# VectorE on constant addresses, one relu per 16 rows: a change beside a full DMA queue

## The chip, the cores and the metric

One core of one Trainium2 chip. The metric is device time in microseconds (us). A profiled run also has a span, from the first to the last instruction of the core that the profile shows; the time is longer than the span, by 1.30 to 1.73 us in the means below, and the difference of the two matters in this case. Every run quoted here was in the fast state, at a granted clock of 1.0.

## The reference

RMSNorm with relu, 16 x 1024 rows of 512 fp32 elements:

```
rms = sqrt(mean(x ** 2, axis=-1) + eps)
out = maximum(x / rms * gamma, 0)
```

33.5 MB are read and 33.5 MB written; per element there is a handful of operations.

## The kernel before

Rows are cut into eight chunks of 16 rows for each of the 128 partitions (4.19 MB), which share six slots in SBUF. SP issues all loads and stores in one queue, in this order: chunks 0 to 5 in, 0 and 1 out, 6 and 7 in, 2 to 7 out. ScalarE squares and sums each row, and takes a root for each eight rows. VectorE makes the factor, multiplies row by row, and clamps. ScalarE and VectorE run loops with addresses in registers. (`take` waits for a semaphore and counts it down in one instruction of its own, in the trace one `EVENT_SEMAPHORE` of 21 ns on VectorE.)

```
    with nc.vector.Fori(0, ngroups) as gi:            # 16 groups of 8 rows
        take(nc.vector, sq, 1)
        base = nc.vector.snap((gi % (nslots * per)) * (G * d))
        col = nc.vector.snap(gi * G)
        ...
        nc.vector.reciprocal(out=rstd[...], in_=rms[...]).then_inc(sv, 1)
        take(nc.vector, sv, 1)
        for j in range(G):
            row = slots[:, bass.ds(base + j * d, d)]
            r = nc.vector.scalar_tensor_tensor(out=row, in0=row, scalar=rstd[...], in1=gamma_sb, ...)
            if j == 0: r.then_inc(tick1, 1)
            if j == 2: r.then_inc(tick3, 1)
            ...
        take(nc.vector, sv, 1)
        nc.vector.tensor_scalar_max(out=blk, in0=blk, scalar1=0.0).then_inc(done, 1)
```

SP does not release a store as soon as its chunk is done, but at two moments that VectorE's rows mark, the ticks:

```
    nc.sync.wait_ge(tick3, 6)          # third row of the sixth group
    store(0)
    store(1)
    for s in range(2):
        nc.sync.wait_ge(sem_slot[s], 32)
        load(7 + s)                    # chunks 6 and 7
    nc.sync.wait_ge(tick1, 11)         # first row of the eleventh group
    for i in range(2, nchunks):
        store(i)
```

## Time and profile before

| | before |
|---|---|
| time, median of 4 runs of the comparison | 160.62 us |
| span of the profiled run | 159.3 us |
| DMA: share of 16 engines, mean rate | 98.2%, 421 GB/s |
| VectorE, ScalarE busy | 126.0 us, 86.3 us |
| last clamp ends, last store issued | 146.44, 146.47 us |

### The profile page before, as it was taken

The numbers are of one execution on the slowest core, as the hardware profiler recorded it, in microseconds if no ns is written. First come the engines' busy times: TensorE is split into PE (matmuls) and PEld (weight loads), VectorE is DVE, ScalarE is ACT, GpSimd is POOL, SyncE is SP. The second block draws the span as 40 slices with busy tenths as digits, with TensorE's granted clock in tenths as the row PEclk, the third lists the DMA queues.
The fourth block names the chain that finished last, engine by engine and source line by source line (L and its number), as shares of the span: only waits on it lengthen the run. The fifth ranks groups of instructions, "written<-read, shape, count | busy, mean of one in ns | idle before, by whom it ended". The sixth has DMA issues, their size and how long they took to land. (4 is left out here: it accounts for less than half of the span.)

```text
span 159.3 us, 999 instructions
## 1 busy us (share of the span) xinstructions
DVE 126.0 (79%) x164; ACT 86.3 (54%) x273; POOL 0.2 (0%) x4
## 2 busy tenths in 40 slices
DVE  1012989898999999999999999999999989897000
ACT  0388929889989988988920098898500000000000
POOL 0000000000000000000000000000000000000000
DMA  6999999999999999999999999999999999999995
GB/s 193 405 453 424 502 395 395 502 420 395 453 469 395 395 502 420 395 428 494 395 395 444 461 411 395 486 436 395 453 453 403 411 494 411 403 461 453 395 420 247
DMA packets 2456, 67.12 MB, mean 421 GB/s; under 512 B 276, under 2 KB 276, under 8 KB 280
## 3 DMA queue, kind: packets, MB, share of 16 engines
q1 hardware_dynamic: 2448, 67.11, 98.2%
q10 hardware_dynamic: 8, 0.01, 0.0%
HBM read 33.56 MB, written 33.55 MB: 421 GB/s over the span
## 5 line engine op out<-in xcount | busy, mean ns | idle before, releaser
L157 DVE SCALAR_TENSOR_TENSOR slots<-slots,rstd,gamma_sb 128x512 f32 x128 | 86.2, 747 | 4.8 <-DVEq L83 4.8
L136 ACT ACTIVATE junk<-slots 128x512 f32 x128 | 74.4, 581 | 20.6 <-ACTq L83 20.3
L167 DVE TENSOR_SCALAR slots<-slots x16 | 36.7, 2294 | 2.4 <-DVEq L83 0.2
L136 ACT ACTIVATION_READ_ACCUMULATOR junk<-slots x128 | 23.9, 187 | 0.0
L152 DVE RECIPROCAL rstd<-rms x16 | 3.1, 197 | 5.3 <-DVEq L83 5.3
L142 ACT ACTIVATE rms<-ss,eps_sb x16 | 4.8, 301 | 3.0 <-ACTq L83 3.0
L146 DVE LOAD_MASK_SELECT gamma_sb<-gseed x1 | 0.0, 14 | 5.4 <-DVEq L83 5.4
L129 ACT ACT_TABLE_LOAD x1 | 1.3, 1283 | 4.2 <-issue 4.2
L122 DVE MEMSET gseed<- 128x512 f32 x1 | 0.5, 485 | 2.6 <-PEq L98 2.6
L146 DVE STREAM_SHUFFLE gamma_sb<-gseed 128x512 f32<-128x512 f32 x1 | 0.7, 723 | 0.0
L190 POOL MEMSET const-bfloat16-1.0<- 128x1 bf16 x1 | 0.1, 102 | 0.0
L190 POOL MEMSET const-uint8-127<- 128x1 uint8 x1 | 0.1, 102 | 0.0
L190 POOL MEMSET const-float32-0.0<- 128x1 f32 x1 | 0.1, 99 | 0.2 <-issue 0.2
L190 POOL MEMSET const-float32-1.0<- 128x1 f32 x1 | 0.1, 99 | 0.0
L123 DVE MEMSET eps_sb<- 128x1 f32 x1 | 0.1, 59 | 0.0
## 6 DMA issues: line engine op xcount, KB each, us to landing
out_dram<-slots SPq DMA_DIRECT2D x8, 4096.0 KB, 20.6
slots<-in_x_dram SPq DMA_DIRECT2D x7, 4096.0 KB, 29.7
slots<-in_x_dram SPq DMA_DIRECT2D x2, 2048.0 KB, 9.7
gseed<-in_gamma_dram ACTq DMA_DIRECT2D x1, 8.0 KB
```

Source lines behind the costliest of these rows:

```text
L122: nc.vector.memset(gseed, 0.0).then_inc(sem_z, 1)
L123: nc.vector.memset(eps_sb, eps).then_inc(sem_z, 1)
L129: nc.scalar.preload_act_table(ACTF.Sqrt)
L136: a = nc.scalar.activation(out=junk[:, j, :], in_=slots[:, bass.ds(base + j * d, d)], func=ACTF.Square, accum_out=ss[:, bass.ds(col + j, 1)])
L142: nc.scalar.activation(out=rms[:, bass.ds(col, G)], in_=ss[:, bass.ds(col, G)], func=ACTF.Sqrt, bias=eps_sb, scale=inv_d).then_inc(sq, 1)
L146: nc.vector.stream_shuffle(gamma_sb, gseed, [0] * 32)
L152: nc.vector.reciprocal(out=rstd[:, bass.ds(col, G)], in_=rms[:, bass.ds(col, G)]).then_inc(sv, 1)
L157: r = nc.vector.scalar_tensor_tensor(out=row, in0=row, scalar=rstd[:, bass.ds(col + j, 1)], in1=gamma_sb, op0=ALU.mult, op1=ALU.mult)
L167: nc.vector.tensor_scalar_max(out=blk, in0=blk, scalar1=0.0).then_inc(done, 1)
L190: nc = _bacc.Bacc("TRN2", target_bir_lowering=False, num_devices=1)
```

## The change

VectorE's rows go to constant addresses: all six slots are written out, and a loop of two turns runs them (in the second turn only slots 0 and 1). Factors are made by 16 rows except in these two slots, and the clamp covers 16 rows (chunk 2 keeps two of eight). The ticks become single marks on chosen rows. The seed memset goes to GpSimd. ScalarE's loop leaves chunks 5 and 7 to constant code. Both programs are now long (VectorE's from 45 to 142 instructions, ScalarE's from 50 to 135), and an alignment (`addr_align`) stands before each.

```
+    for engine in (nc.scalar, nc.vector):
+        engine.addr_align(256, offset=128, max_nops=0)
...
-    nc.sync.wait_ge(tick3, 6)
+    nc.sync.wait_ge(tick, 1)
...
-    nc.sync.wait_ge(tick1, 11)
+    nc.sync.wait_ge(tick, 2)
...
-    nc.vector.memset(gseed, 0.0).then_inc(sem_z, 1)
+    nc.gpsimd.memset(gseed, 0.0).then_inc(sem_z, 1)
...
-    with nc.vector.Fori(0, ngroups) as gi:
-        ... (the loop above)
+    with nc.vector.Fori(0, 2) as o:
+        chunk_rows(0, by_group=True)
+        chunk_rows(1, by_group=True)
+        one = steps
+        with nc.vector.If_lt(nc.vector.to_reg(o), 1):
+            chunk_rows(2, clamps=(G, K), ticked=13)
+            chunk_rows(3)
+            chunk_rows(4)
+            chunk_rows(5, ticked=6)
+            ...
```

(`chunk_rows(s)` writes out the reciprocal, 16 row operations and the clamp of slot s; `ticked` is the row that marks the tick; waits now stand on the operation itself.)

More of the change, by code (lines that the diff above doesn't have):

```diff
@@ L37 @@
     nslots = 6
-    ngroups = rows // G
     per = K // G
@@ L64 @@
     sq = nc.alloc_semaphore("sq")
-    tick1 = nc.alloc_semaphore("tick1")
-    tick3 = nc.alloc_semaphore("tick3")
+    tick = nc.alloc_semaphore("tick")
     done = nc.alloc_semaphore("done")
@@ L85, in store @@
     def store(i):
-        nc.sync.wait_ge(done, per * (i + 1))
+        nc.sync.wait_ge(done, i + 1)
         nc.sync.dma_start(out=ov[i], in_=slot_ap(i)).then_inc(sem_slot[i % nslots], 16)
-    ctx.enter_context(tc.manual_schedule(engines={mybir.EngineType.SP}))
+    ctx.enter_context(tc.manual_schedule(engines={
+        mybir.EngineType.SP, mybir.EngineType.Activation, mybir.EngineType.DVE}))
+    for engine in (nc.scalar, nc.vector):
+        engine.addr_align(256, offset=128, max_nops=0)
     early = 2
@@ L110 @@
         load(7 + s)
-    nc.sync.wait_ge(tick1, 11)
+    nc.sync.wait_ge(tick, 2)
     for i in range(2, nchunks):
         store(i)
+    nc.gpsimd.memset(gseed, 0.0).then_inc(sem_z, 1)
+    nc.gpsimd.memset(eps_sb, eps).then_inc(sem_z, 1)
     for m, (i, a, r) in enumerate(loads):
@@ L120 @@
         nc.gpsimd.sem_inc(ready, r // G)
-    nc.vector.memset(gseed, 0.0).then_inc(sem_z, 1)
-    nc.vector.memset(eps_sb, eps).then_inc(sem_z, 1)
     nc.scalar.wait_ge(sem_z, 1)
@@ L130 @@
     take(nc.scalar, sem_z, 2)
-    with nc.scalar.Fori(0, ngroups) as gi:
-        take(nc.scalar, ready, 1)
-        base = nc.scalar.snap((gi % (nslots * per)) * (G * d))
-        col = nc.scalar.snap(gi * G)
-        for j in range(G):
-            a = nc.scalar.activation(
-                out=junk[:, j, :], in_=slots[:, bass.ds(base + j * d, d)],
-                func=ACTF.Square, accum_out=ss[:, bass.ds(col + j, 1)])
-            if j == G - 1:
-                a.then_inc(sa, 1)
-        take(nc.scalar, sa, 1)
-        nc.scalar.activation(out=rms[:, bass.ds(col, G)], in_=ss[:, bass.ds(col, G)],
-                             func=ACTF.Sqrt, bias=eps_sb, scale=inv_d).then_inc(sq, 1)
@@ L145, with square @@
-    take(nc.vector, sem_g, 16)
-    nc.vector.stream_shuffle(gamma_sb, gseed, [0] * 32)
-    with nc.vector.Fori(0, ngroups) as gi:
-        take(nc.vector, sq, 1)
-        base = nc.vector.snap((gi % (nslots * per)) * (G * d))
-        col = nc.vector.snap(gi * G)
-        blk = slots[:, bass.ds(base, G * d)]
-        nc.vector.reciprocal(out=rstd[:, bass.ds(col, G)],
-                             in_=rms[:, bass.ds(col, G)]).then_inc(sv, 1)
-        take(nc.vector, sv, 1)
-        for j in range(G):
-            row = slots[:, bass.ds(base + j * d, d)]
+    def square(row, col, j):
+        return nc.scalar.activation(out=junk[:, j, :], in_=slots[:, bass.ds(row, d)],
+                                    func=ACTF.Square, accum_out=ss[:, bass.ds(col, 1)])
@@ new lines, in root, with chunk_sums @@
+    def root(col, r):
+        return nc.scalar.activation(out=rms[:, bass.ds(col, r)], in_=ss[:, bass.ds(col, r)],
+                                    func=ACTF.Sqrt, bias=eps_sb, scale=inv_d)
+    def chunk_sums(i):
+        c = (i % nslots) * K
+        take(nc.scalar, ready, per)
+        for j in range(K):
+            a = square((c + j) * d, c + j, j % G)
+            if j % G == G - 1:
+                a.then_inc(sa, 1)
+                nc.scalar.wait_ge(sa, (j + 1) // G)
+        root(c, K).then_inc(sq, per)
+        nc.scalar.sem_inc(sa, -per)
@@ new lines @@
+    with nc.scalar.Fori(0, 2) as o:
+        with nc.scalar.Fori(o * 12, o * 4 + 10) as gi:
+            take(nc.scalar, ready, 1)
+            col = nc.scalar.snap((gi % (nslots * per)) * G)
+            base = nc.scalar.snap(col * d)
+            for j in range(G):
+                a = square(base + j * d, col + j, j)
+            a.then_inc(sa, 1)
+            take(nc.scalar, sa, 1)
+            root(col, G).then_inc(sq, 1)
+        with nc.scalar.If_lt(nc.scalar.to_reg(o), 1):
+            chunk_sums(5)
+        with nc.scalar.Else():
+            chunk_sums(7)
@@ new lines, with factors, clamp, chunk_rows @@
+    nc.vector.wait_ge(sem_g, 16)
+    nc.vector.stream_shuffle(gamma_sb, gseed, [0] * 32)
+    steps = 0
+    def factors(c, r, n):
+        nc.vector.wait_ge(sq, n)
+        nc.vector.reciprocal(out=rstd[:, c:c + r], in_=rms[:, c:c + r]).then_inc(sv, 1)
+        nonlocal steps
+        steps += 1
+        nc.vector.wait_ge(sv, steps)
+    def clamp(c, r):
+        blk = slots[:, c * d:(c + r) * d]
+        return nc.vector.tensor_scalar_max(out=blk, in0=blk, scalar1=0.0)
+    def chunk_rows(s, by_group=False, clamps=(K,), ticked=None):
+        nonlocal steps
+        c = s * K
+        for j in range(K):
+            if by_group and j % G == 0:
+                factors(c + j, G, (c + j) // G + 1)
+            elif j == 0:
+                factors(c, K, per * (s + 1))
+            row = slots[:, (c + j) * d:(c + j + 1) * d]
@@ L157 @@
             r = nc.vector.scalar_tensor_tensor(
-                out=row, in0=row, scalar=rstd[:, bass.ds(col + j, 1)], in1=gamma_sb,
+                out=row, in0=row, scalar=rstd[:, c + j:c + j + 1], in1=gamma_sb,
                 op0=ALU.mult, op1=ALU.mult)
-            if j == 0:
-                r.then_inc(tick1, 1)
-            if j == 2:
-                r.then_inc(tick3, 1)
-            if j == G - 1:
-                r.then_inc(sv, 1)
-        take(nc.vector, sv, 1)
-        nc.vector.tensor_scalar_max(out=blk, in0=blk, scalar1=0.0).then_inc(done, 1)
@@ L169 @@
-    take(nc.sync, done, ngroups)
-    take(nc.sync, tick1, ngroups)
-    take(nc.sync, tick3, ngroups)
+            if j == ticked:
+                r.then_inc(tick, 1)
+            if j + 1 in clamps:
+                r.then_inc(sv, 1)
+                steps += 1
+                nc.vector.wait_ge(sv, steps)
+                k = clamps.index(j + 1)
+                n = j + 1 - (clamps[k - 1] if k else 0)
+                b = clamp(c + j + 1 - n, n)
+        b.then_inc(done, 1)
+    with nc.vector.Fori(0, 2) as o:
[7 more added lines that the diff above has]
+            chunk_rows(5, ticked=6)
+            nc.vector.sem_inc(sq, -nslots * per)
+            nc.vector.sem_inc(sv, -steps)
@@ L172 @@
+    take(nc.sync, done, nchunks)
+    take(nc.sync, tick, 2)
+    take(nc.sync, sem_g, 16)
+    take(nc.sync, sq, 2 * per)
+    take(nc.sync, sv, one)
     for i in range(nchunks - nslots, nchunks):
```

## The prediction

> **What bounds the kernel now.** I read the page's slices and queue table first, since they say which resource never rests, then the groups of instructions, then the waits of the DMA queue's engine (SP), and last the timeline of the tail.
>
> ```profile
> span 159.3 us, 999 instructions
> DVE 126.0 (79%) x164; ACT 86.3 (54%) x273; POOL 0.2 (0%) x4
> DMA  6999999999999999999999999999999999999995
> GB/s 193 405 453 424 502 395 395 502 420 395 453 469 395 395 502 420 395 428 494 395 395 444 461 411 395 486 436 395 453 453 403 411 494 411 403 461 453 395 420 247
> q1 hardware_dynamic: 2448, 67.11, 98.2%
> L157 DVE SCALAR_TENSOR_TENSOR slots<-slots,rstd,gamma_sb 128x512 f32 x128 | 86.2, 747 | 4.8 <-DVEq L83 4.8
> L167 DVE TENSOR_SCALAR slots<-slots x16 | 36.7, 2294 | 2.4 <-DVEq L83 0.2
> L152 DVE RECIPROCAL rstd<-rms x16 | 3.1, 197 | 5.3 <-DVEq L83 5.3
> ```
>
> The DMA row is 9 in all 40 slices but the first and the last, and the load/store queue has 98.2% of sixteen engines' time. The sawtooth of GB/s between 395 and 502 is packets being booked to the slice in which they start; over a long stretch it evens out, as the windows view shows:
>
> ```profile
> 0.00:8.00 8.00, 0.49 (x2) 1.28 (x1) 0.20 (x4) 1.00 0.78 300
> 8.00:58.00 50.00, 41.72 (x56) 42.70 (x137) 0.00 (x0) 1.00 1.01 435
> 102.00:146.00 44.00, 41.62 (x53) 10.93 (x35) 0.00 (x0) 1.00 1.01 438
> ```
>
> (Columns: stretch, length, busy us of VectorE, ScalarE and GpSimd with counts, clock, DMA share, GB/s.) The DMA share is full in the middle. Every byte is needed: 33.56 MB in, 33.55 MB out. So the DMA engines set the time, if they are never left without work. VectorE is at 79%, but a busy share does not show whether the last store waited for it. For that, the tail and SP's waits:
>
> ```profile
> 144.15 2.29 DVE L167 TENSOR_SCALAR slots<-slots  x1
> 146.47 0.33 SPq L87 DMA_DIRECT2D out_dram<-slots  x1
> ```
> ```profile
> SPq L83 <- SPq L83: 12.0, 2, 9.7
> ```
>
> VectorE's last clamp ends at 146.44 and store 7 is issued at 146.47, so that store did wait for VectorE. But was the queue empty? SP's last two waits (12.0 us together, the longest 9.7) are for stores 6 and 7. The span ends with the second, so store 6 landed at about 159.3 - 9.7 = 149.6. Store 7 was queued 3.1 us before store 6 had landed and took 9.7 us behind it: 4.19 MB in 9.7 us is 432 GB/s, the full rate again. The last store stood in the queue, not VectorE on the path. (The chain view names the last clamp for 1.4% of the span only; it is blind to a full queue.)
>
> [...] the clamp does 4096 elements in 2.29 us, the two-tensor row operation 512 in 0.75. [...] in the trace of before, no instruction packet lies after the span's start, so its loops cause none.
>
> **The change part by part.** One step of eight rows on VectorE, from the timeline of before:
>
> ```profile
> 22.74 0.20 DVE L152 RECIPROCAL rstd<-rms  x1
> 23.23 5.39 DVE L157 SCALAR_TENSOR_TENSOR slots<-slots,rstd,gamma_sb 128x512 f32 x8 [0.30 <-DVEq L83]
> 28.77 2.29 DVE L167 TENSOR_SCALAR slots<-slots  x1
> 30.98 0.20 DVE L152 RECIPROCAL rstd<-rms  x1
> ```
>
> Start to start: reciprocal to first row 0.49; a row (5.39 - 0.747)/7 = 0.663; last row to clamp 28.77 - 23.23 - 7 x 0.663 = 0.90; clamp to next reciprocal 2.21. A step is 8.24, sixteen are 131.9, and 14.48 (first reciprocal) + 131.9 = 146.4: the timeline's end, so VectorE is self-paced all the way.
>
> - Constant addresses remove eight register instructions a step. The trace has seven of them running ahead behind the first rows, hidden; only the one between wait and first row (115 ns) is exposed. So the row pitch stays 0.663, and reciprocal to first row falls to about 0.38. I choose 0.85 for last row to clamp, as the wait joins the clamp itself.
> - Factors: twelve reciprocals in place of sixteen (two in each of chunks 0, 1, 6 and 7, whose slots are the first two; one in chunks 2 to 5).
> - Clamps: nine in place of sixteen. A 16-row one should take 2.21 + 4096 x 0.52 ns = 4.34: the elements stay, only a wait and a start go.
> - Chunks 0, 1, 6, 7: 2 x 0.38 + 15 x 0.663 + 0.85 + 4.34 = 15.9 each, 63.6 in all. Chunk 2: 0.38 + 14 x 0.663 + 2 x 0.85 + 2 x 2.21 = 15.8. Chunks 3 to 5: 0.38 + 15 x 0.663 + 0.85 + 4.34 = 15.5 each, 46.5 in all. Sum 125.9: VectorE saves 6.0 us and ends at about 140.4.
> - ScalarE's two constant chunks save little, and ScalarE is not short: 0.61 us a row, 16 rows in about 11.5 us, under the 15.5 of VectorE. Chunk 2 now wants both of its roots at once. By ScalarE's pace of before the second ends at 45.9; VectorE arrives at about 46.3. No wait, narrowly. The second factor of chunk 0 is wanted at 20.2 and its root ends at 20.0: at most 0.1 us.
> - The seed memset goes to GpSimd. Gamma is shuffled at 8.4 and first needed at 15.0; a few us later would still be hidden.
>
> What reaches the end? Store 7 is issued 6 us earlier, into a queue that was already full. Saving: nothing. What could reach it is the moment of the first stores, which SP delays until the ticks:
>
> ```profile
> 58.30 0.82 SPq L87 DMA_DIRECT2D out_dram<-slots  x2
> 71.23 10.35 SPq L77 DMA_DIRECT2D slots<-in_x_dram  x2
> 98.19 48.62 SPq L87 DMA_DIRECT2D out_dram<-slots  x6
> ```
>
> The queue then runs dry near 61 and 100. The ticks move to row 14 of chunk 2 and row 7 of chunk 5. By my sums the first fires at 14.5 + 31.8 + (0.38 + 7 x 0.663 + 0.85 + 2.21) + 5 x 0.663 + 0.75 = 58.4, the second at 14.5 + 31.8 + 15.8 + 31.0 + 0.38 + 6 x 0.663 + 0.75 = 98.2. They are aimed at the old moments: more rows on a faster VectorE give the same time. So the order and moment of the first stores are as before, and the estimate is zero change: 160.5.
>
> **The rivals.** (1) *VectorE sets the end*, and its 6.0 us become 3 or more: about 155. For it, store 7 goes out straight after the last clamp; against it, 3.1 us of queue and 9.7 us at full rate, and the bytes alone: 67.11 MB at 435 GB/s are 154.3 us, to which a first packet near 1.7 and the half-empty end have to be added. (2) *A tick comes too late*, by a slower VectorE or a wait for a 16-row root, and the queue runs dry: each us of lateness costs up to a us. If my row pitch were off by 1%, the second tick would move by 0.6 us; SP needed 1.0 us from first issue (0.73) to first packet (1.75), so there is little in reserve. That gives 161 or so. (3) *Fetching instructions*: the longer program, or the jump over the alignment padding, adds packets to one DMA engine or stalls VectorE. [...] a fetch at the start is hidden behind the loads. At worst some tenths. (4) *Slow packets at the start become fewer*: the first slice has only 193 GB/s, about a us lost; but the change leaves the first two loads and their barrier alone.
>
> **Range and chances.** The floor leaves no way to 157.3 (2% faster), and the dry-queue rival would need 3.2 us of gap for 2% slower. Runs of before span 160.47 to 160.72. I take 160.1 to 161.0: 0.4 down for a tidier queue end, 0.5 up for a late tick or a fetch.
>
> **What would show it.** Right: VectorE busy 122 to 124 us in fewer instructions, rows still at 0.66 us pitch, its end near 140, SP's stores at about 58.4 and 98.2, store 7 issued near 140, SP's last wait still 9.7 us, DMA share 98%, and the span within 0.4 us of 159.3. Wrong: a DMA slice below 9 in the middle (ticks), a wait of VectorE for a root at chunk 2, or a last wait of SP different from 9.7 us. A span under 158.5 would mean that the queue had hidden gaps that I took for full use.

(Cut marks stand where a passage said of the hardware what no trace or run of this case shows. No term of the sum is cut: it came to 125.9 us from VectorE's first reciprocal to its end, 6.0 us saved there, and zero change of the time, 160.5 us. Its rate for the longer clamp, 0.52 ns an element, is not in the trace of before, where every clamp has 4096 elements; the trace after shows it: 4426 ns for 8192 elements against 2294 for 4096, so 2132 ns for 4096 more. That the queue runs dry near 61 and 100 us fits the loads of chunks 5 and 7, done at 61.56 and 100.54 us in the kernel before. That a late tick costs up to its lateness, and that a fetch at the start is hidden, were estimates: in e13 a first tick 0.73 us later made the span 1.0 us longer, and what fetches cost is measured below.)

## The result, and the profile after

The changed kernel takes **161.42 us** (median of 4 runs, 161.22 to 161.52) against **160.62 us** before (160.47 to 160.97). The ratio is 1.0045, 95% interval 1.0025 to 1.0065: slower clear of noise, and outside the predicted range. A ratio is the mean time of one kernel's fast runs over that of the other's of the same rounds, so not quite the ratio of the medians.

The page of the changed kernel:

```profile
span 159.7 us, 714 instructions
DVE 124.0 (78%) x151; ACT 85.7 (54%) x271; POOL 0.8 (0%) x6
DMA  6999999999999999999999999999999999999993
q1 hardware_dynamic: 2448, 67.11, 98.0%
q14 instruction: 2, 0.02, 0.0%
DVE 55%; issue 3%; ACT 0%; DVEq 0%; ACTq 0%
L182 DVE TENSOR_SCALAR slots<-slots 128x8192 f32<-128x8192 f32 (+1 forms) x9 | 35.6, 3952 | 0.3
L175 DVE RECIPROCAL rstd<-rms 128x8 f32<-128x8 f32 (+1 forms) x12 | 2.6, 214 | 5.9 <-ACT rms L140 5.9
```

Two of these lines mislead and one tells. The chain of work now claims 55% for VectorE, though its last work ends 20 us before the span does. The DMA row looks as it did. The new line is `q14 instruction`: two packets of 8192 bytes, which the kernel before did not have in its span. It has 0.0% of the engines' time.

VectorE did what it was meant to do. Its timeline, one chunk:

```profile
15.01 0.20 DVE L175 RECIPROCAL rstd<-rms 128x8 f32<-128x8 f32 x1 [5.45 <-ACT rms L140]
15.24 5.39 DVE L193 SCALAR_TENSOR_TENSOR slots<-slots,rstd,gamma_sb 128x512 f32<-128x512 f32 x8
20.83 0.20 DVE L175 RECIPROCAL rstd<-rms 128x8 f32<-128x8 f32 x1 [0.19 <-ACT rms L140]
21.07 5.39 DVE L193 SCALAR_TENSOR_TENSOR slots<-slots,rstd,gamma_sb 128x512 f32<-128x512 f32 x8
26.50 4.43 DVE L182 TENSOR_SCALAR slots<-slots 128x8192 f32<-128x8192 f32 x1
```

Eight rows still take 5.39 us; reciprocal to first row is 0.23 in place of 0.49. And the tail, with SP's wait for its last two stores:

```profile
135.06 4.43 DVE L182 TENSOR_SCALAR slots<-slots 128x8192 f32<-128x8192 f32 x1
139.51 0.33 SPq L88 DMA_DIRECT2D out_dram<-slots  x1
```
```profile
SPq L84 <- SPq L84: 19.2, 2, 9.7
```

Store 7 is issued 7 us earlier, and again lands 9.7 us behind store 6. The gain stood in the queue, as foreseen. So where do 0.8 us come from? At the start, ScalarE's first square, which waits for the first half of chunk 0, comes 0.75 us later (first line before, second line after):

```profile
8.73 0.60 ACT L136 ACTIVATE junk<-slots 128x512 f32 x1 [3.27 <-ACTq L83]
```
```profile
9.48 0.60 ACT L136 ACTIVATE junk<-slots 128x512 f32 x1 [3.96 <-ACTq L84]
```

The trace's semaphore records say why. Each transfer's semaphore is raised sixteen times, which I read as once by each DMA engine. The median, the last but one and the last of the sixteen, in us:

```
transfer                 before                    after
chunk 0, first half      7.84   8.11   8.26        7.88   8.16   9.01
chunk 0, second half    12.69  12.96  13.00       12.74  12.98  13.71
load of chunk 5         61.27  61.52  61.56       61.32  61.55  62.29
load of chunk 7        100.22 100.45 100.54      100.18 100.42 101.54
store 2                109.89 110.17 110.46      109.91 110.15 111.25
store 7                158.18 158.53 159.23      158.19 158.75 159.63
```

The typical engine is where it was, to 0.05 us, from the first transfer to the last. **One** engine (the same one, as I read it; these records name none) is about 0.75 us later than the last one of before from the first half of chunk 0 on, and 1.0 us later at the load of chunk 7; the work that waits for a transfer starts behind its last engine: the first square 0.47 us after the sixteenth raise in both kernels (8.73 for 8.26, 9.48 for 9.01). By store 7 the difference has shrunk to 0.40 us, which is that of the two profiled spans: in the kernel before, too, one engine falls behind while the stores run, to 1.05 us behind the median. The two instruction packets start at 1.8 us (578 ns) and 3.8 us (328 ns), and a load packet that starts at 4.1 us takes 1125 ns instead of 611.

A second part is outside the span. Time minus span is 1.59 us in the changed kernel's four runs (1.52 to 1.67), and 1.33 in the kernel before (mean of 11 runs). One more 8192-byte instruction packet stands at 161.1 us, after the span's end. The 0.8 us are so about 0.5 in the span (159.8 against 159.3, medians of the runs) and 0.26 after it.

### The profile page after: what moved, and what is told of

Same layout as the page of the kernel before. It is cut to its first block, busy times and chain, and to the rows that moved or that the text cites. A ratio compares the mean times of both kernels' runs of the same rounds, so it can differ in the third digit from the quotient of the medians.

```text
span 159.7 us, 714 instructions
## 1 busy us (share of the span) xinstructions
DVE 124.0 (78%) x151; ACT 85.7 (54%) x271; POOL 0.8 (0%) x6
## 4 chain that ended last, share of the span: by engine, by line
DVE 55%; issue 3%; ACT 0%; DVEq 0%; ACTq 0%
DVE slots L193 40%; DVE slots L182 14%; DVE rstd L175 1%; ACT rms L140 0%; DVEq L207 0%; ACTq L140 0%; DVEq L217 0%
## 5 line engine op out<-in xcount | busy, mean ns | idle before, releaser
L193 DVE SCALAR_TENSOR_TENSOR slots<-slots,rstd,gamma_sb 128x512 f32<-128x512 f32 x128 | 86.0, 748 | 0.4
L136 ACT ACTIVATE junk<-slots 128x512 f32 (+1 forms) x128 | 74.5, 582 | 21.3 <-ACTq L84 20.8
L182 DVE TENSOR_SCALAR slots<-slots 128x8192 f32<-128x8192 f32 (+1 forms) x9 | 35.6, 3952 | 0.3
L136 ACT ACTIVATION_READ_ACCUMULATOR junk<-slots (+1 forms) x128 | 23.9, 187 | 0.0
L175 DVE RECIPROCAL rstd<-rms 128x8 f32<-128x8 f32 (+1 forms) x12 | 2.6, 214 | 5.9 <-ACT rms L140 5.9
L140 ACT ACTIVATE rms<-ss,eps_sb (+1 forms) x14 | 4.2, 302 | 2.4 <-ACTq L84 2.2
L119 POOL MEMSET gseed<- 128x512 f32 x1 | 0.5, 524 | 1.9 <-POOLq L102 1.9
```

Source lines behind the costliest of these rows:

```text
L119: nc.gpsimd.memset(gseed, 0.0).then_inc(sem_z, 1)
L136: return nc.scalar.activation(out=junk[:, j, :], in_=slots[:, bass.ds(row, d)], func=ACTF.Square, accum_out=ss[:, bass.ds(col, 1)])
L140: return nc.scalar.activation(out=rms[:, bass.ds(col, r)], in_=ss[:, bass.ds(col, r)], func=ACTF.Sqrt, bias=eps_sb, scale=inv_d)
L175: nc.vector.reciprocal(out=rstd[:, c:c + r], in_=rms[:, c:c + r]).then_inc(sv, 1)
L182: return nc.vector.tensor_scalar_max(out=blk, in0=blk, scalar1=0.0)
```

## The experiments

Theory F: instruction fetches, at the start by one DMA engine, and at the end after the span. Rivals: P, VectorE's new pace or the new program as such; C or T, the moments of the ticks. Sixteen kernels, five rounds each, each beside runs of the kernel before on the same chip. All gave correct results.

| run | time | before | ratio (95%) | span | time - span |
|---|---|---|---|---|---|
| changed kernel | 161.42 | 160.62 | 1.0045 (1.0025-1.0065) | 159.8 | 1.59 |
| e1 changed, no alignment | 161.88 | 160.66 | 1.0065 (1.0052-1.0078) | 160.6 | 1.30 |
| e2 before + alignments | 160.67 | 160.66 | 1.0003 (0.9990-1.0015) | 159.4 | 1.32 |
| e3 changed, VectorE aligned only | 161.43 | 160.66 | 1.0044 (1.0031-1.0057) | 159.9 | 1.57 |
| e4 changed, ScalarE aligned only | 161.82 | 160.66 | 1.0064 (1.0051-1.0077) | 160.5 | 1.30 |
| e5 before, ticks early | 161.14 | 160.72 | 1.0024 (1.0011-1.0038) | 159.8 | 1.34 |
| e6 changed, both ticks late | 162.36 | 160.72 | 1.0092 (1.0078-1.0105) | 160.6 | 1.67 |
| e7 changed, both ticks early | 162.99 | 160.72 | 1.0142 (1.0126-1.0157) | 161.5 | 1.62 |
| e8 short program | 161.16 | 160.72 | 1.0031 (1.0017-1.0045) | 159.4 | 1.71 |
| e9 short program, aligned | 161.10 | 160.73 | 1.0017 (1.0004-1.0030) | 159.8 | 1.31 |
| e10 short program, inner loop | 166.50 | 160.73 | 1.0364 (1.0351-1.0377) | 165.2 | 1.31 |
| e11 before + tail on VectorE | 161.15 | 160.73 | 1.0021 (1.0008-1.0034) | 159.4 | 1.73 |
| e12 before + fetch in the stream | 161.24 | 160.73 | 1.0031 (1.0018-1.0044) | 159.9 | 1.33 |
| e13 changed, first tick late | 162.48 | 160.57 | 1.0114 (1.0099-1.0129) | 160.8 | 1.68 |
| e14 changed, second tick late | 160.96 | 160.57 | 1.0023 (1.0009-1.0037) | 159.3 | 1.65 |
| e15 e2, first tick earlier | 160.81 | 160.57 | 1.0018 (1.0005-1.0032) | 159.5 | 1.33 |
| e16 e9, second tick later | 160.96 | 160.57 | 1.0030 (1.0016-1.0045) | 159.6 | 1.32 |

(Spans are medians of the runs of that kernel, recorded to 0.1 us, and the last column has means; the kernel before has 159.3, 159.4, 159.4 and 159.2 in the four groups, and 1.31 to 1.33 after the span.)

### e1, e3, e4: the alignments taken away

```
e1  -    for engine in (nc.scalar, nc.vector):
    -        engine.addr_align(256, offset=128, max_nops=0)
e3  -    for engine in (nc.scalar, nc.vector):
    +    for engine in (nc.vector,):
e4  -    for engine in (nc.scalar, nc.vector):
    +    for engine in (nc.scalar,):
```

> The changed kernel without the two address alignments (ScalarE and VectorE); nothing else differs. Theory F (instruction fetch): the jumps over the padding cause the two 8 KB instruction packets at 1.8 and 3.8 us, both on one DMA engine, which then runs 0.6 to 0.7 us behind the other fifteen, and a third packet after the end. Expected: no instruction packet at the start, chunk 0's second half complete at 13.0 instead of 13.7, span 159.3, time 160.6. Theory T (the ticks leave the queue dry): time stays at 161.4. Theory P (the rest of the new program, its length or its loops, costs the time): stays at 161.2 or more, and fetches may turn up in the middle.

> The changed kernel with the alignment on VectorE alone. Theory F: one packet at the start in place of two, the one DMA engine about 0.3 to 0.6 us late; time between 160.6 and 161.4, near 161.0; whether the packet after the end goes or stays tells which engine causes it. Theories T and P: 161.4.

> The changed kernel with the alignment on ScalarE alone. Theory F: one packet at the start, time near 161.0, and e3 and e4 together make up the loss of both alignments. Theories T and P: 161.4.

A miss, and a useful one. Without the alignments the kernel is slower, not faster. The packets did not vanish: they moved to 46.2 us, when VectorE goes on to the code of slot 2, and to 74.1 us, when ScalarE is in its constant chunk. e4, with VectorE alone unaligned, has the one at 46.2; e3, with ScalarE alone unaligned, has one at 75.3. In the four long programs (changed, e1, e3, e4) the fetch comes in any case; the alignment only chooses its moment. The runs also part the two packets at the start: with VectorE's alone (e3, 3.8 us) the first half of chunk 0 ends at 9.02, with ScalarE's alone (e4, 1.8 us) at 8.07. So the late engine at the start is due to VectorE's fetch.

ScalarE's fetch in the middle leaves the span where it was (159.9). With VectorE's in the middle the span is longer (160.5 in e4 against 159.8), but the fetch is not alone in this: the data are not late at the start, so the ticks come 0.65 us earlier (58.10 and 97.37), and ticks matter, as shown below. What the fetch itself costs I read from the packet records, which name no engine: in e4 a load packet that starts at 46.6 us, as the fetch ends, takes 1875 ns instead of 1213. If it would have started where the fetch did, 0.3 us earlier, that is 0.97 us for a fetch that itself took 325 ns. The last engine finished load 7 at 102.53 (median engine 100.16) and store 7 at 160.62 (158.22); 0.6 us of this lag came with load 5 and 0.8 with load 7, where stores begin.

The last column moves in its own way: 1.30 where VectorE is not aligned, 1.57 to 1.59 where it is.

### e2: the alignments alone, on the kernel before

```
+    for engine in (nc.scalar, nc.vector):
+        engine.addr_align(256, offset=128, max_nops=0)
```

> The kernel before with nothing but the two alignments (and the manual schedule of three engines that comes with them). Theory F: two instruction packets at the start, one DMA engine late by 0.6 to 0.7 us, time 161.2 to 161.5. Theories T and P: 160.6, as before.

A miss again. The two packets are there (1.8 and 3.7 us), and one engine is as late as in the changed kernel: the first half of chunk 0 ends at 8.98, the typical engine at 7.80. Yet the span is 159.4 and the time that of before. So a late engine at the start does not by itself make a late end. What else, then? Its ticks are tied to VectorE's rows and moved along with the late data, to 59.0 and 98.9 us; those of the changed kernel are at 58.75 and 98.03. That made the ticks the next suspects.

### e5, e6, e7: the ticks moved

```
e5 (before)   tick3 on row j == 0 of its group, not 2
              tick1 on row j == 6 of group 10, not row 0 of group 11
e6 (changed)  ticked=14 for chunk 2 (was 13), ticked=7 for chunk 5 (was 6)
e7 (changed)  ticked=11 for chunk 2,          ticked=3 for chunk 5
```

> The kernel before with both ticks earlier: stores 0 and 1 released at about 57.0 us instead of 58.3, stores 2 to 4 at about 94 instead of 98.2. No other part of the change. Theory C (a store issued while loads are still in the queue costs one DMA engine 0.4 to 0.9 us; the changed kernel's moments are a little early or unlucky): span 159.7 to 160.6, time 161.0 to 162. Theory F (only instruction fetches cost time): span 159.3, time 160.6 to 160.7.

> The changed kernel with each tick one row later (stores 0 and 1 at 59.4 us, stores 2 to 4 at 98.7, as late as in the kernel before with the alignments, which lost nothing). Theory C: span falls from 159.8 to about 159.4, time to about 161.0 (the 0.26 us after the span stay). Theory F: 161.4 unchanged.

> The changed kernel with the ticks earlier: stores 0 and 1 at about 57.4 us, stores 2 to 4 at about 96.0. Theory C: span 160.2 or more, time 161.8 or more. Theory F: 161.4 unchanged.

Ticks matter in either direction. Earlier ones cost the kernel before 0.4 us of span (e5) and the changed kernel 1.7 (e7); in e5 it is the typical engine that is late, with store 7 done at 158.89 where before has 158.18. But later ones, which I expected to help, cost the changed kernel 0.8 (e6). Two ticks moved at once: e13 and e14 part them below.

### e8 to e10: the new pace in a short program

In e8 the changed schedule (one clamp per 16 rows, memset on GpSimd) is a loop over chunks with register addresses, ScalarE has its old loop, nothing is aligned. e9 adds the alignments; e10 puts the rows into an inner loop of eight, to have fewer instructions. "Theory E" of e10 and e11 was made from e8: a VectorE program longer than some length, 63 instructions in e8 against 45 before, costs time after the span (0.38 us in e8).

```
e8  +    with nc.vector.Fori(0, nchunks) as ci:
    +        col = nc.vector.snap((ci % nslots) * K)
    +        ... (16 rows by register, ticks on rows 14 and 3, one clamp)
e9  +    for engine in (nc.scalar, nc.vector):
    +        engine.addr_align(256, offset=128, max_nops=0)
    -            if j == 3:          # the second tick
    +            if j == 2:
e10 +        with nc.vector.Fori(0, per) as h:      # inside the loop over chunks
```

> The changed kernel's schedule in a short program: one relu per 16 rows on VectorE and the seed memset on GpSimd stay, but the rows use register addresses in a loop over chunks, ScalarE keeps its loop, no alignment; ticks set for 57.8 and 98.5 us. No instruction fetch should be seen after the start. Theory F: span 159.3, time 160.6, and the difference of time and span back at 1.32 us, although VectorE ends some 3 us earlier than before. Theory P (a VectorE that is ahead, or the 16-row relu, costs the DMA engines time): 161 or more.

> The short program of e8 with the two alignments added and the second tick one row earlier, so that its moments are near those of the changed kernel (58.4 and 98.3 us after the expected 0.6 us of delay). Theory F1 (the fetch at the start makes one DMA engine late, and this is the 0.5 us in the span): two instruction packets at the start, span about 159.8 to 159.9 against 159.4 of e8; time minus span back to 1.3 us[...]. Theory C (the ticks' moments alone): span 159.4.

> The short program with an inner loop over eight rows: 51 VectorE instructions in the program in place of 63 (before 45, changed 142). Still one relu per 16 rows. Theory E[...]: time minus span between 1.3 and 1.7 us, 1.3 if 51 still fit; span 159.4, so the time 160.7 if it fits.

e8 has no instruction packet in its span, VectorE ends early (its last clamp starts at 139.03), and the span is 159.4, as before. So the pace, the 16-row clamp and the memset on GpSimd are innocent: rival P falls for the span. e9 differs by the alignments and one row of a tick: its engine is late again (9.02 for the first half of chunk 0, median 7.84), and the span is 159.8. That is the cost of the fetches in this schedule, 0.4 us, with the ticks where they then fall (58.41 and 98.25; in e8 57.85 and 98.34).

The last column was a surprise: 1.71 for e8, though its VectorE program is only 18 instructions longer than that of the kernel before; aligned, in e9, it is back at 1.31. It fits a cost of the length and place of VectorE's program, which e11 tests.

e10 is a miss of another kind. Its 51 instructions leave 1.31 us after the span, but its VectorE stalls in the inner loop:

```profile
L173 DVE RECIPROCAL rstd<-rms x16 | 3.2, 200 | 12.0 <-DVEq L86 12.0
```

12.0 us idle ahead of the reciprocals, where e8 has 4.7. Of the 12.0, 4.6 are the first wait, as in e8; the rest is eight stalls of 0.92 us at the second half of each chunk. Another 3.9 us lie ahead of the clamps. The ticks, tied to VectorE, came at 61.4 and 104.9 us, where the kernel before has its loads of chunks 5 and 7 done at 61.56 and 100.54; so, as I read it, the queue ran dry: a span of 165.2. It says nothing on the fetches in the span, but it shows that VectorE does set the end when it is late.

### e11, e12: one suspect each, on the kernel before

```
e11 +    for k in range(18):
    +        nc.vector.memset(pad[:, k:k + 1], 0.0)     # after VectorE's last loop
e12 -    with nc.vector.Fori(0, ngroups) as gi: ...
    +    steps(0, 4)                                    # the same loop, in two parts
    +    nc.vector.addr_align(256, offset=128, max_nops=0)
    +    steps(4, ngroups)
```

> The kernel before with 18 memsets of one column of a scratch tile on VectorE after its last loop (63 instructions in the program, as in e8); they run beside the last store. Theory E: span 159.4 unchanged, time minus span rises from 1.33 to about 1.7 us, time 161.0 to 161.1. If the 0.38 us of e8 had another cause (GpSimd's memset, the earlier end of VectorE): 160.7.

> The kernel before with VectorE's loop cut in two after four groups (about 47 us) and an alignment between, so that one fetch of instructions falls into the full stream of loads. No other part of the change. Theory F: one instruction packet near 47 us, one DMA engine late by about 0.7 to 1 us from there, span 160.0 to 160.6, time 161.3 to 161.9. If a fetch in the stream is harmless: 160.7.

Both as expected, e12 at the low end. In e11 eighteen tiny memsets, run beside the last store, leave the span at 159.4 and add 0.42 us after it: 1.73 against 1.31. They take 0.30 us in all, from 146.2 us on, 13 us before the span ends, so their number counts and not their work. In e12, a single fetch in the stream:

```profile
q14 instruction: 1, 0.01, 0.0%
```

It starts at 49.8 us and makes one engine late: load 4 is done at 52.48 (before, 51.85), load 5 at 62.55 (median 61.33; before, 61.56 and 61.27). The span is 159.9, 0.5 us longer; apart from the fetch, only the code of the loop stands twice. (The profile is that of the fastest of the five runs, with a span of 159.5; the others have 159.8 to 160.0. Its ticks, at 58.02 and 97.90, are 0.3 us earlier than in the profile of before, but so are those of e11, 58.12 and 98.00, which lost nothing in the span.)

### e13 to e16: ticks against a late engine

```
e13 (changed)  ticked=14 for chunk 2, second tick as it was
e14 (changed)  ticked=7 for chunk 5,  first tick as it was
e15 (e2)       tick3 on row j == 1, not 2
e16 (e9)       second tick on row j == 3, not 2
```

> The changed kernel with the first tick alone a row later (stores 0 and 1 at 59.4 us). If e6 lost its 0.8 us at the first change from loads to stores, span 160.6 again; if at the second, 159.8 as the changed kernel.

> The changed kernel with the second tick alone a row later (stores 2 to 4 at 98.7 us). If the changed kernel's loss on the late DMA engine near 98 us comes from releasing these stores while that engine still loads, span 159.4 to 159.5; if the start's delay alone counts, 159.8; if e6's loss is here, 160.6.

> The kernel before with the alignments (e2, which lost only 0.1 us in the span) and the first tick a row earlier: stores 0 and 1 at 58.4 us in place of 59.0, the moment of the kernel before. If e2 was spared because its ticks moved later along with its late data, the span rises to about 159.8; if not, it stays at 159.4.

> The short aligned program of e9 (span 159.8) with the second tick a row later (98.9 us, the moment of e2). If that moment spares the late DMA engine, span 159.4; if the start's delay alone counts, 159.8.

e14 is the answer for the span. Its stores, as SP issued them, ahead those of the changed kernel, then those of e14:

```profile
58.75 0.82 SPq L88 DMA_DIRECT2D out_dram<-slots  x2
98.03 41.82 SPq L88 DMA_DIRECT2D out_dram<-slots  x6
```
```profile
58.76 0.82 SPq L88 DMA_DIRECT2D out_dram<-slots  x2
98.69 41.16 SPq L88 DMA_DIRECT2D out_dram<-slots  x6
```

With the second tick one row later, everything else equal, fetches and late engine included (9.03 for the first half of chunk 0), the span falls to 159.3 (five runs, 159.1 to 159.4; the changed kernel's four have 159.7 to 159.9), against 159.2 of the kernel before in the same rounds. The semaphore records show where. How far the last engine is behind the median, in us, and when SP released the stores (one profile of each):

```
           load 4  load 5  load 6  load 7  store 7   stores released
before       0.28    0.29    0.32    0.33     1.05   58.30, 98.19
changed      0.96    0.97    0.96    1.37     1.44   58.75, 98.03
e14          1.01    1.10    1.27    1.27     0.93   58.76, 98.69
e9           1.00    1.60    1.59    1.59     1.57   58.41, 98.25
```

In the changed kernel the late engine loses 0.4 us more at load 7, where stores 2 to 4 come in; in e14 it loses nothing there. In the changed kernel's packets one load packet, at 99.4 us, takes 1.77 us instead of 1.21; e14 has none over 1.3 us near that moment. What is left of e14's loss, 0.39 us in time, is nearly all after the span (0.33). So the fetch makes one engine late, and the moment of the stores decides what that costs. I know no rule for the moment: e9 loses 0.6 us with its first stores, released at 58.41, and nothing with the second at 98.25.

e13 shows the opposite edge. With the first tick at 59.5 us, all engines lose, after the change from stores to loads near 80 us; the windows view of the changed kernel, then of e13:

```profile
62.00:98.00 36.00, 35.83 (x46) 23.31 (x75) 0.00 (x0) 1.00 1.01 432
```
```profile
62.00:98.00 36.00, 35.82 (x46) 22.26 (x72) 0.00 (x0) 1.00 1.00 416
```

16 GB/s less over 36 us is some 1.3 us of transfer by this count, which books packets by their start; the median engine ends load 6 1.0 us later (91.44 against 90.47). Between 76 and 83 us, 24 packets take over 1.3 us, against five in the changed kernel. So e6's loss is at the first tick, and its later second tick was the better half.

e15 and e16 are weaker. Giving e2 an earlier first tick costs 0.1 to 0.2 us (159.5 against 159.2 of before, where e2 had 159.4 against 159.3); e16's later second tick gains perhaps 0.2 on e9 (159.6 against 159.8), not the 0.4 that I expected. The direction agrees with e14, the size is near the spread of the runs. The table above says why e16 had so little to gain: e9 loses nothing at the second release.

## Why the prediction was wrong, point by point

- **The DMA engines set the time, and a faster VectorE gains nothing.** Right: e8 has the pace and keeps the span (159.4 us).
- **The size of VectorE's saving.** Predicted 125.9 us from first reciprocal to end, measured 139.49 - 15.01 = 124.5. The row pitch held; reciprocal to first row is 0.23 (I had 0.38), last row to clamp 0.78 (0.85). The wait itself on the operation is cheaper than I chose: the first row starts 36 ns after the reciprocal has ended and the clamp 34 ns after the last row, where the kernel before has 298 and 157 ns. Most of those gaps were the separate instructions for the wait (21 ns) and, ahead of the first row, for the register (115 ns), and the time between them.
- **"So the order and moment of the first stores are as before, and the estimate is zero change."** This failed. The moments came out as worked out, 58.75 and 98.03 for 58.4 and 98.2. But the data were not as before: one of sixteen DMA engines was 0.75 us late, and against that engine the second moment was too early. One row later (e14), the span is that of before to 0.1 us. That the moments came out so near was partly luck: VectorE began 0.53 us later than before (15.01 for 14.48) and waited for roots, which its quicker steps made up for.
- **"A fetch at the start is hidden behind the loads. At worst some tenths."** This is the step that failed first. There is nothing to hide behind: the DMA share is 1.01 from 8 to 58 us, and, as I read the records, the fetch uses one of the engines that carry the loads (behind it a load packet takes 1125 ns instead of 611 in the changed kernel, 1875 instead of 1213 in e4, and one of the sixteen raises is 0.6 to 1 us later than in the kernel before). I judged it by its share of the traffic. VectorE did not stall: in e1, with the fetch at 46.24 us, reciprocal to first row is 0.29 us (46.01 to 46.30), as in the changed kernel without it (46.74 to 47.03). A single fetch costs the span 0.5 us in e12; the pair at the start 0.4 in e9, 0.5 in the changed kernel, and 0.1 in e2 and in e14, whose second tick is later (98.90 and 98.69).
- **What I did not think of:** the end of the program. Some lengths and places of VectorE's program cost time after the span: 0.26 us in the changed kernel, 0.38 to 0.42 in e8 and e11. Unaligned, 51 instructions (e10, 1.31) cost nothing, 63 (e8, e11) do, and some 141 (e1, e4, 1.30) do not; aligned, the short program (e9, 1.31) costs nothing and the long one does (e3, 1.57). By what rule is not shown: no trace shows the addresses. No view of the span shows the cost; only the time beside the span does.
- **The check that I named** (last wait of SP 9.7 us, DMA share 98%, span within 0.4 of 159.3) was passed by a kernel that is 0.8 us slower. It was blind to one late engine. One named sign of being wrong did appear: VectorE waited 0.29 us for chunk 2's root at 46.74 us, where I had "no wait, narrowly". It moved VectorE, which had time to spare.
- **A small misreading in rival 4.** The first slice (3.98 us at 193 GB/s) loses 2.2 us of full rate, not about one; 1.75 of them lie before the first packet.

What stays open: why a store released a few rows too early, or the first pair 0.7 us too late, slows packets at all. The traces show where (near 60, 80 and 100 us, where loads and stores change over) and in which packets, not by what mechanism. Why e2's late engine does not fall further behind by the end is argued from its ticks, not shown in full by e15. And the packet after the end is in the records of five kernels, each time 1.4 us after the span. In e7 it is missing, and the profiled run is the only one of e7's four with a short time after the span (1.36 us), which fits; but e8 and e11 have the long time (1.7 us) without it. So that it is the cause of the 0.3 to 0.4 us is an inference. That the length and place of VectorE's program is the cause is shown: by e11 in the kernel before, and by e1 and e4 (1.30 us without VectorE's alignment) in the changed one.

No version here beats the kernel before: e2 ties with it, e14 comes nearest of those with the long program (1.0023). The kernel before, too, ends with one engine 1.05 us behind the median; whether that can be gained, no run shows.

## What to carry to other kernels

Where the DMA queue is full, count the instructions of each engine's program before writing a loop out, and look for instruction packets: in e12 a single fetch ended load 5 0.99 us later (62.55 against 61.56), with its median engine 0.06 us later, and made the span 0.5 us longer. Compare median and last completion of a transfer; the busy share of sixteen engines (98.2% before, 98.0% after) did not show the one that was late. When anything delays the data, aim the moments at which stores are released again (one row later made the span 1.0 us longer in e13 and 0.5 us shorter in e14), and look at time minus span as well as at the span (0.26 of the 0.8 us here).
